# Expert routing in a Hyena and mixture-of-experts layer: where the first weight split runs, where one of three counts runs, and where the first transposes land

## The chip, the cores and the metric

One core of a Trainium2 chip runs the whole program in one launch. The metric is the device time of one execution in microseconds (us), lower is better. Three executions of the kernel before the change took 4108.78, 4110.93 and 4116.41 us; the median is 4110.93.

## The reference, cut to what matters

The program is one layer of a trunk over 2048 latent tokens of width 1024: a Hyena long convolution, a residual and a norm, then a mixture of 16 experts in which each expert chooses its tokens. The change touches the beginning of the second half, which computes this:

```
aff = softmax(h @ w_router)                    # 2048 tokens x 16 experts
gate, idx = top_k(transpose(aff), 256)         # each expert takes its 256 best tokens
xe = h[idx]                                    # gather
ye = (silu(xe @ w1) * (xe @ w3)) @ w2 * gate   # per expert, d_ff = 2048
out[idx] += ye                                 # scatter-add
```

All inputs and outputs are float32.

## The kernel before

**Order of the work.** The layer's first half ends in `phase_out`, which writes the normed tokens to `xnd` in HBM and leaves the logits `lg` in SBUF (128 partitions x 16 token groups x 16 experts). `phase_route` finds each expert's 256th best score. `phase_moe` then runs the experts one after the other.

**Routing.** `lg` becomes the softmax scores: a maximum, a subtraction, Exp on ACT (L1307), a sum, a division. The scores are transposed, so that 128 partitions hold 16 experts in slices, and are taken as two 16-bit halves `vs[1]` (upper) and `vs[0]` (lower). The 256th best is found two bits at a time, from above: 7 steps on the upper half, 8 on the lower. In a step three candidates `cand` are tried: for each, a count on DVE of the entries that are not below it (L1340, 128x256, with an accumulator), then one matmul with the 0/1 matrix `blkb` that adds up the partitions of an expert (L1342), then on DVE the three sums are compared with the capacity (L1358) and the next candidates are formed (L1362). Beside that DVE keeps the threshold `thr` (L1348) and the base of the next candidates (L1355). A step begins when the step before has its `cand`, so the 15 steps form a chain. After them come a running count along the tokens (L1379), two matmuls, and the table `tab` of slots.

**First expert.** `route(0)` makes a one-hot matrix, multiplies it with the table (L1484), computes the token numbers `idx`, and issues two gathers on POOL's queue (L1492, 128 rows of 4 KB each, `xg0` and `xg1`). In four rounds the gathered tokens are transposed on PE into one PSUM bank `tp` (four 128x128 transposes a round, L1502), ACT writes the upper part of the split (`xs` L1504) and DVE the rest (L1505).

**Weights.** Every float32 matrix is split into an upper and a lower part: ACT casts the upper part (`w1h`, `w3h`, `w2h`, L1420), another engine subtracts (`w1l`, `w3l`, `w2l`, L1421). An expert's weights come in 8 chunks of three 1 MB loads (w1, w3, w2) on SP's queue (L1411); raw w1 and w3 have two buffers, raw w2 has one, the split parts have two. `moe_start` loads chunks 0 and 1 of expert 0 ahead, and there the subtraction runs on POOL: all six 128x2048 subtractions stand on POOL's queue beside the steps of the routing. For all later chunks it runs on DVE.

**Experts.** In a chunk, `project` forms two groups of 16 matmuls for each half `i` into the banks `ab` (three of them; L1522, L1523), `hidden` splits the product into `hh` and `hl` (L170, L171), and `back` multiplies it by w2 into four accumulator banks (L175 to L177). Outside the parts under `manual_schedule` a list scheduler fixes the order of the instructions on each engine.

Of the kernel before, what the change touches and what calls it, by code (L numbers as in the profile page):

```python
# [12 lines left out]
F32 = mybir.dt.float32  # L13
F32R = mybir.dt.float32r
BF16 = mybir.dt.bfloat16
I32 = mybir.dt.int32
U16 = mybir.dt.uint16
AF = mybir.ActivationFunctionType
OP = mybir.AluOpType
# [4 lines left out]
T = 2048  # L24
# [26 lines left out]
def f_(ap):  # L51
    return ap.bitcast(F32)
# [1241 lines left out]
def phase_route(tc, ident, ones_f, lg, R):  # L1294
# [6 lines left out]
    with ExitStack() as st:  # L1301
        wk = st.enter_context(tc.tile_pool(reuse_waits="tile", name="r_wk", bufs=1))
        ps = st.enter_context(tc.tile_pool(reuse_waits="tile", name="r_ps", bufs=1, space=PSUM))
        mx = wk.tile([128, 16], F32, name="mx")
# [20 lines left out]
        for h in (1, 0):  # L1325
# [10 lines left out]
            for n in steps:  # L1336
                cnt = wk.tile([128, 3], BF16, name="cnt", bufs=2)
                for k in range(3):
                    junk = wk.tile([128, 256], U16, name=f"junk{k}")
                    nc.vector.tensor_scalar(junk, v, cand[:, k:k + 1], 0.0, op0=OP.is_ge, op1=OP.add, accum_out=cnt[:, k:k + 1])  # L1340
                p = ps.tile([128, 3], F32, name="cp", bufs=2)
                nc.tensor.matmul(p, lhsT=blkb, rhs=cnt, start=True, stop=True)  # L1342
# [15 lines left out]
                nc.vector.tensor_scalar(ge, p, CAP - 0.5, 0.0, op0=OP.is_ge, op1=OP.add, accum_out=num)  # L1358
# [37 lines left out]
def moe_start(tc, A, st, R):  # L1396
# [46 lines left out]
    for n in range(8):  # L1443
        for k in range(3):
            nc.gpsimd.memset(R.kc[:, n, k:k + 1], float((k + 1) << (14 - 2 * n)))
# [6 lines left out]
    R.first = []  # L1452
    for n in range(2):
        R.first.append(split(raws, nc.gpsimd))
        if n == 0:
            raws = load(0, 1)
# [3 lines left out]
def phase_moe(tc, A, rowd, ident, ones_f, lg, R, xnd, accd, out):  # L1460
    nc = tc.nc
    tab, lo, hi, slot, spf = R.tab, R.lo, R.hi, R.slot, R.spf
    with ExitStack() as st:
# [7 lines left out]
        def route(e):  # L1471
# [25 lines left out]
            for q in range(4):  # L1497
                p = ps.tile([128, 2, 256], F32, name="tp", bufs=1)
                for i in range(2):
                    k = 2 * q + i  # L1500
                    for h in range(2):
                        nc.tensor.transpose(out=p[:, i, h * 128:h * 128 + 128], in_=xg[h][:, k * 128:k * 128 + 128], identity=ident)  # L1502
                xh, xl = (xs[:, 2 * q:2 * q + 2, c] for c in range(2))
                nc.scalar.copy(xh, p)  # L1504
                nc.vector.tensor_tensor(xl, p, f_(xh), OP.subtract)  # L1505
                yield
# [102 lines left out]
        with tc.manual_schedule():  # L1609
            for _ in route(0):  # L1610
                pass
# [10 lines left out]
        for e in range(NE - 3):  # L1622
            idx, gate, x = nxt
            acc = [[pa.tile([128, 512], F32, name=f"acc{h}{q}") for q in range(2)] for h in range(2)]
            for fc in range(8):
                ws = R.first.pop(0) if R.first else R.split(R.load(e, fc))
# [202 lines left out]
```

## Time and profile before

The profile below is of one execution of its own.

| | |
|---|---|
| profiled execution | 4111.43 us, of which the span of the profile is 4109.3 us |
| median of three executions | 4110.93 us |
| PE busy | 3840.9 us, 93% of the span |
| DVE busy | 2810.4 us, 68% |
| ACT busy | 1964.7 us, 48% |
| POOL busy | 1092.5 us, 27% |
| granted TensorE clock, mean | 0.972 of 2.4 GHz |
| the 15 routing steps, first count to last matmul | 1801.79 to 1852.86 us of the span |

How to read it: a span time counts from the first instruction. A timeline row gives start, duration, engine, line, operation and, in square brackets, the time that the engine stood idle before it and what ended that. A group row gives the count, the busy time, the mean in ns of one and the idle time before.

### The profile page before, as it was taken

To read this page: it belongs to the slowest core of one execution; us is meant where nothing else is said; L and a number is where in the kernel's file an instruction comes from. 1 tells how busy PE (TensorE), PEld (TensorE's weight loads), DVE (VectorE), ACT (ScalarE), POOL (GpSimd) and SP (SyncE) were. 2 spreads that over 40 slices of the span, in tenths; PEclk is the share of its full clock that TensorE was granted. 3 is DMA by queue.
4 is the path that set the end of the run, shared out by engine and by line. 5 is a ranking of instruction groups with operands and counts; after the bars stand their busy time and mean duration, and the time that the engine had idled before them with its cause. 6 is when DMAs were issued, how large, how long until landed. Compare 5 with 4: busy or idle time off the path is not lost.

```text
span 4109.3 us, 53113 instructions
## 1 busy us (share of the span) xinstructions
PE 3840.9 (93%) x19879; PEld 3185.1 (78%) x19879; DVE 2810.4 (68%) x4018; ACT 1964.7 (48%) x2886; POOL 1092.5 (27%) x1132
## 2 busy tenths in 40 slices
PE   5899999998999998948999999999999999999997
PEld 3666766777777887736888888888888888888896
DVE  5777876776877877785666666666666666656766
ACT  3544543333777652123555555555555555544443
POOL 2355552212577542130000000000000000015635
PEclk8899999999999999968999999999999999999999
DMA  6355656666989995444666666666666666656764
GB/s 200 116 171 171 179 168 210 221 205 220 272 264 268 269 283 190 150 159 149 195 198 202 205 195 198 202 205 195 199 204 205 195 198 207 204 186 213 239 229 161
DMA packets 620797, 831.75 MB, mean 202 GB/s; under 512 B 56627, under 2 KB 506947, under 8 KB 618236
## 3 DMA queue, kind: packets, MB, share of 16 engines
q1 hardware_dynamic: 545594, 661.93, 50.3%
q0 software_dynamic: 57088, 163.48, 13.5%
q10 hardware_dynamic: 17858, 2.95, 0.5%
q8 instruction: 157, 2.57, 0.3%
q14 instruction: 100, 0.82, 0.1%
HBM read 643.82 MB, written 150.75 MB: 193 GB/s over the span
## 4 chain that ended last, share of the span: by engine, by line
PE 72%; DVE 8%; issue 6%; DMA 5%; POOL 4%; ACT 4%; SPq 0%; ACTq 0%; POOLq 0%; DVEq 0%
PE ab L1522 19%; PE ab L1523 10%; PE acc L175 5%; PE acc L176 5%; PE acc L177 5%; PE ip L175 3%; PE ip L177 3%; PE ip L176 3%; PE sp L335 2%; PE op L175 1%; PE op L177 1%; PE op L176 1%; PE xp L857 1%; PE ab L177 1%; PE ab L176 1%
## 5 line engine op out<-in xcount | busy, mean ns | idle before, releaser
L1522 PE MATMUL ab<-xs,w3h 128*128 128x512 f32 x1664 | 600.7, 400 | 0.0
L1522 PE MATMUL ab<-xs,w1h 128*128 128x512 f32 x1664 | 598.3, 399 | 0.0
L1421 DVE TENSOR_TENSOR w2l<-w2r,w2h 128x2048 fp32r<-128x2048 f32 x126 | 297.6, 2362 | 267.2 <-ACT w2h L1420 267.2
L1523 PE MATMUL ab<-xs,w3l 128*128 128x256 f32 x1664 | 468.3, 281 | 0.0
L1523 PE MATMUL ab<-xs,w1l 128*128 128x256 f32 x1664 | 466.6, 280 | 0.0
L175 PE MATMUL acc<-w2h,hh 128*128 128x512 f32 x1024 | 404.2, 395 | 14.7 <-ACT hh L170 13.8
L176 PE MATMUL acc<-w2l,hh 128*128 128x512 f32 x1024 | 402.5, 393 | 0.0
L177 PE MATMUL acc<-w2h,hl 128*128 128x512 f32 x1024 | 399.7, 391 | 0.8 <-DVE hl L171 0.8
L1522 PEld LDWEIGHTS ab<-xs,w3h 128*128 128x128 f32 x1664 | 313.0, 188 | 76.6
L1522 PEld LDWEIGHTS ab<-xs,w1h 128*128 128x128 f32 x1664 | 313.1, 188 | 73.0
L1568 POOL DMA_INDIRECT accd<-y,idx x27 | 68.5, 2536 | 1102.4 <-DVE y L1562 1096.1
L1421 DVE TENSOR_TENSOR w1l<-w1r,w1h 128x2048 fp32r<-128x2048 f32 x126 | 300.9, 2388 | 62.6 <-ACT w1h L1420 62.4
L170 ACT CAST hh<-u 128x256 fp32r<-128x256 f32 x256 | 104.1, 407 | 478.9 <-DVE u L1545 478.9
L1523 PEld LDWEIGHTS ab<-xs,w1l 128*128 128x128 f32 x1664 | 314.2, 189 | 7.1
L1523 PEld LDWEIGHTS ab<-xs,w3l 128*128 128x128 f32 x1664 | 314.8, 189 | 0.0
L1526 DVE TENSOR_TENSOR u<-ab,u 128x256 f32<-128x256 f32 x416 | 174.6, 420 | 204.9 <-ACT u L1525 196.5
L1421 DVE TENSOR_TENSOR w3l<-w3r,w3h 128x2048 fp32r<-128x2048 f32 x126 | 292.9, 2324 | 19.0 <-ACT w3h L1420 19.0
L1420 ACT CAST w2h<-w2r 128x2048 fp32r<-128x2048 f32 x128 | 244.1, 1907 | 95.3 <-PE acc L177 86.5
L1420 ACT CAST w1h<-w1r 128x2048 fp32r<-128x2048 f32 x128 | 244.5, 1910 | 80.0 <-PE ab L1522 78.9
L1420 ACT CAST w3h<-w3r 128x2048 fp32r<-128x2048 f32 x128 | 244.7, 1912 | 68.3 <-PE ab L1522 66.3
L175 PE MATMUL ip<-hh,wh 128*128 128x512 f32 x576 | 239.5, 416 | 2.7 <-ACT hh L170 2.7
L1525 ACT COPY u<-ab 128x256 f32<-128x256 f32 x416 | 153.0, 368 | 184.2 <-PE ab L1523 184.0
(409 smaller groups left out, 9245.2 us busy)
## 6 DMA issues: line engine op xcount, KB each, us to landing
w1r<-in_moe_w_dram SPq DMA_DIRECT2D x128, 1024.0 KB
w3r<-in_moe_w_dram SPq DMA_DIRECT2D x128, 1024.0 KB
w2r<-in_moe_w_dram SPq DMA_DIRECT2D x128, 1024.0 KB
fud<-ev SPq DMA_DIRECT2D x128, 256.0 KB
kr<-fud SPq DMA_DIRECT2D x64, 512.0 KB
bn<-ao POOLq DMA_DIRECT2D x248, 128.0 KB, 7.1
win<-in_c_win_dram SPq DMA_DIRECT2D x64, 256.0 KB
mw<-in_mod_w_dram SPq DMA_DIRECT2D x64, 256.0 KB
```

Source lines behind the costliest of these rows:

```text
L170: nc.scalar.copy(hi, raw)
L175: nc.tensor.matmul(out, lhsT=ah, rhs=bh, start=start, stop=False)
L176: nc.tensor.matmul(out, lhsT=ah, rhs=bl, start=False, stop=False)
L177: nc.tensor.matmul(out, lhsT=al, rhs=bh, start=False, stop=stop)
L335: nc.tensor.matmul(p, lhsT=s1[:, th], rhs=hb[th], start=True, stop=(n0 > 0))
L1420: nc.scalar.copy(h, raw)
L1421: eng.tensor_tensor(l, raw, f_(h), OP.subtract)
L1522: nc.tensor.matmul(p, lhsT=ws[2 * j][:, k, fs], rhs=xs[:, k], start=(k == 0), stop=False)
L1523: nc.tensor.matmul(p[:, 0], lhsT=ws[2 * j + 1][:, k, fs], rhs=xs[:, k, 0], start=False, stop=(k == 7))
L1525: nc.scalar.copy(u, p[:, 1])
L1526: nc.vector.tensor_tensor(u, p[:, 0], u, OP.add)
L1568: nc.gpsimd.indirect_dma_start(out=accd, out_offset=at(idx, h), in_=y, in_offset=None, compute_op=OP.add)
```

## The change

Five edits, all in the routing and in the first chunk of expert 0.

1. POOL no longer subtracts for chunks 0 and 1. Chunk 0's three subtractions run on DVE (as `scalar_tensor_tensor`), called by `R.rest()` behind the issue of the first gathers; chunk 1 is loaded there and split like all later chunks.
2. In each step two counts stay on DVE, now of the entries below the candidate. The third is on ACT: the sign of (candidate - value), summed over the row by the accumulator. The third candidate is lowered by one half so that no difference is zero.
3. The step has two matmuls, one for ACT's sum and one for DVE's two counts, into columns of one bank; the comparison uses a tile of limits `lim` that POOL fills once.
4. `route(0)` puts the first round of transposes into `tp` and the other three into the three banks `ab`.
5. The first chunk takes its split weights from `R.first`, the second its loads from `R.second`.

```diff
+        lim = wk.tile([128, 3], F32, name="lim")
+        nc.gpsimd.memset(lim[:, 0:2], T - CAP + 0.5)
+        nc.gpsimd.memset(lim[:, 2:3], T - 2.0 * CAP + 1.0)
...
-                cnt = wk.tile([128, 3], BF16, name="cnt", bufs=2)
-                for k in range(3):
+                cnt = wk.tile([128, 2], BF16, name="cnt", bufs=2)
+                cs = wk.tile([128, 1], BF16, name="cs", bufs=2)
+                sign = wk.tile([128, 256], BF16, name="sign")
+                with nc.allow_low_precision(reason="whole numbers of at most 256"):
+                    nc.scalar.activation(sign, v, AF.Sign, scale=-1.0, bias=cand[:, 2:3], accum_out=cs)
+                for k in range(2):
                     junk = wk.tile([128, 256], U16, name=f"junk{k}")
-                    nc.vector.tensor_scalar(junk, v, cand[:, k:k + 1], 0.0, op0=OP.is_ge, op1=OP.add, accum_out=cnt[:, k:k + 1])
+                    nc.vector.tensor_scalar(junk, v, cand[:, k:k + 1], 0.0, op0=OP.is_lt, op1=OP.add, accum_out=cnt[:, k:k + 1])
                 p = ps.tile([128, 3], F32, name="cp", bufs=2)
-                nc.tensor.matmul(p, lhsT=blkb, rhs=cnt, start=True, stop=True)
+                nc.tensor.matmul(p[:, 2:3], lhsT=blkb, rhs=cs, start=True, stop=True)
+                nc.tensor.matmul(p[:, 0:2], lhsT=blkb, rhs=cnt, start=True, stop=True)
...
-                nc.vector.tensor_scalar(ge, p, CAP - 0.5, 0.0, op0=OP.is_ge, op1=OP.add, accum_out=num)
+                nc.vector.scalar_tensor_tensor(ge, p, 1.0, lim, op0=OP.mult, op1=OP.is_le, accum_out=num)
...
-    R.first = []
-    for n in range(2):
-        R.first.append(split(raws, nc.gpsimd))
-        if n == 0:
-            raws = load(0, 1)
+    hs = [(n, raw, wt.tile(list(raw.shape), F32R, name=n + "h")) for n, raw in raws]
+    for n, raw, h in hs[:2]:
+        nc.scalar.copy(h, raw)
+
+    def rest():
+        nc.scalar.copy(hs[2][2], hs[2][1])
+        for n, raw, h in hs:
+            l = wt.tile(list(raw.shape), F32R, name=n + "l")
+            nc.vector.scalar_tensor_tensor(l, raw, 1.0, f_(h), op0=OP.mult, op1=OP.subtract)
+            R.first += [h, l]
+        R.second = load(0, 1)
...
-                p = ps.tile([128, 2, 256], F32, name="tp", bufs=1)
+                p = ps.tile([128, 2, 256], F32, name="ab", bufs=3) if wide and q else ps.tile([128, 2, 256], F32, name="tp", bufs=1)
...
-            for _ in route(0):
+            first = route(0, wide=True)
+            next(first), next(first)
+            R.rest()
+            for _ in first:
                 pass
```

ACT, from the last activation of `phase_out` to the loads behind the routing, before (the names carry buffer numbers; the first three casts are chunk 0's, the other three chunk 1's):

```order
L1290 ACTIVATE r_15240<-ident_74 128x1
L1307 ACTIVATE lg_8488<-lg_8488 128x256
L1420 CAST w1h_15258<-w1r_15066 128x2048
L1420 CAST w3h_15262<-w3r_15068 128x2048
L1420 CAST w2h_15266<-w2r_15070 128x2048
L1420 CAST w1h_15276<-w1r_15270 128x2048
L1420 CAST w3h_15280<-w3r_15272 128x2048
L1420 CAST w2h_15284<-w2r_15274 128x2048
```

The same place now, up to the third step's sign:

```order
L1290 ACTIVATE r_15240<-ident_74 128x1
L1465 CAST w2h_15263<-w2r_15070 128x2048
L1310 ACTIVATE lg_8488<-lg_8488 128x256
L1462 CAST w1h_15261<-w1r_15066 128x2048
L1462 CAST w3h_15262<-w3r_15068 128x2048
L1344 ACTIVATE sign_15282,cs_15281<-half1_15276,kc_15077 128x256
L1428 CAST w1h_15785<-w1r_15636 128x2048
L1344 ACTIVATE sign_15302,cs_15301<-half1_15276,cand_15298 128x256
L1428 CAST w3h_15789<-w3r_15638 128x2048
L1344 ACTIVATE sign_15321,cs_15320<-half1_15276,cand_15317 128x256
```

The cast of chunk 0's w2, written behind the gathers in the code, stands ahead of Exp (now L1310); chunk 0's other two casts stand ahead of the first step's sign, and chunk 1's w1 and w3 between the signs of steps 1 and 2 and of steps 2 and 3. The cast of chunk 1's w2 is now in the first chunk of expert 0, behind the first Silu.

DVE, from the second `idx` of expert 0 to the first splits of `xs`, now (before, the four `xs` rows followed the row of `gate` at once):

```order
L1504 TENSOR_TENSOR idx_15613<-tp_15612,n2_15615 128x1
L1505 SCALAR_TENSOR_TENSOR jk_15616,gate_15614<-slot_15075,n2_15615,tp_15612 128x16
L1468 SCALAR_TENSOR_TENSOR w1l_15630<-w1r_15066,w1h_15261 128x2048
L1468 SCALAR_TENSOR_TENSOR w3l_15632<-w3r_15068,w3h_15262 128x2048
L1468 SCALAR_TENSOR_TENSOR w2l_15634<-w2r_15070,w2h_15263 128x2048
L1521 TENSOR_TENSOR xs_15642<-tp_15643,xs_15642 128x2x256
```

Three 128x2048 subtractions now stand between the second gather's index and the first `xs`. On PE all 16 transposes of expert 0 now come in one run, followed by the table matmuls of expert 1 (L1500, before inside expert 0's fourth chunk), and only then the first projection; before, the projection's matmuls stood between the rounds of transposes. Behind expert 0's second chunk the order on every engine is as before.

## Rows read from the trace of the kernel before

**Rows 1.** Windows view, busy us (and instructions) of each engine, then PEclk, DMA share, GB/s.

```profile
1870.00:1880.00 10.00, 8.62 (x43) 7.50 (x44) 2.77 (x4) 2.35 (x4) 0.00 (x0) 0.74 0.01 2
...
1940.00:2500.00 560.00, 559.12 (x2967) 476.46 (x2966) 353.94 (x454) 288.54 (x376) 30.97 (x18) 1.00 0.63 201
```

**Rows 2.** Timeline of the first routing step: start us, us, engine, line, operation.

```profile
1801.22 4.52 POOL L1421 TENSOR_TENSOR w1l<-w1r,w1h 128x2048 fp32r<-128x2048 f32 x1 [43.17 <-ACT w1h L1420]
...
1803.34 2.43 DVE L1355 TENSOR_SCALAR base<-kc,thr 128x3 f32<-128x3 f32 x1
```

**Rows 3.** Groups of instructions, 1640 to 1960 us: busy us, mean ns, idle before.

```profile
L1362 DVE SCALAR_TENSOR_TENSOR cand<-num,base 128x3 f32<-128x3 f32 x13 | 10.5, 806 | 0.5
...
L1355 DVE TENSOR_SCALAR base<-kc,thr 128x3 f32<-128x3 f32 x13 | 9.2, 710 | 0.4
...
L1348 DVE SCALAR_TENSOR_TENSOR thr<-num,thr 128x1 f32<-128x1 f32 x13 | 8.1, 624 | 0.0
```

**Rows 4.** Source view of the same three lines: ns min/median/max.

```profile
L1362 DVE SCALAR_TENSOR_TENSOR cand<-num,base x13: 160/161/4356, 1805.9 to 1851.2; 128x3 f32<-128x3 f32 x13
...
L1355 DVE TENSOR_SCALAR base<-kc,thr x13: 98/228/4425, 1803.3 to 1850.8; 128x3 f32<-128x3 f32 x13
...
L1348 DVE SCALAR_TENSOR_TENSOR thr<-num,thr x13: 152/153/3215, 1811.5 to 1852.6; 128x1 f32<-128x1 f32 x13
```

**Rows 5.** Timeline of the fifth routing step, POOL idle.

```profile
1830.85 0.48 DVE L1340 TENSOR_SCALAR_CACHE_REDUCE junk<-half,cand 128x256 uint16<-128x256 uint16 x1
...
1831.26 0.47 DVE L1340 TENSOR_SCALAR_CACHE_REDUCE junk<-half,cand 128x256 uint16<-128x256 uint16 x1
...
1832.20 0.16 PE L1342 MATMUL cp<-cnt,blkb 128*128 128x3 bf16 x1 [1.78 <-DVE junk L1340]
```

**Rows 6.** Timeline: Exp on ACT, the first step's first count on DVE, two casts of chunk 1 on ACT.

```profile
1798.95 0.40 ACT L1307 ACTIVATE lg<-lg 128x256 f32<-128x256 f32 x1
...
1801.79 0.48 DVE L1340 TENSOR_SCALAR_CACHE_REDUCE junk<-half,kc 128x256 uint16<-128x256 uint16 x1
...
1805.86 1.90 ACT L1420 CAST w1h<-w1r 128x2048 fp32r<-128x2048 f32 x1 [1.11 <-DMA w1r<-in_moe_w_dram]
...
1808.86 1.90 ACT L1420 CAST w3h<-w3r 128x2048 fp32r<-128x2048 f32 x1 [1.11 <-DMA w3r<-in_moe_w_dram]
```

**Rows 7.** Groups of instructions on ACT, whole span, shapes kept apart.

```profile
L526 ACT ACTIVATE ht<-g,md 128x256 f32<-128x256 f32 x48 | 24.2, 565 | 18.8 <-DMA h2d<-ht 8.0 <-issue 5.2 <-DVE hl L530 3.5
...
L1290 ACT ACTIVATE r<-ident 128x1 f32<-128x1 f32 x1 | 0.2, 203 | 0.0
```

**Rows 8.** Timeline: the two gathers of expert 0 and the transposes that wait.

```profile
1862.27 1.18 POOL L1492 DMA_INDIRECT xg<-xnd,idx  x1 [34.25 <-DVE jk L1489]
...
1863.76 0.97 POOL L1492 DMA_INDIRECT xg<-xnd,idx  x1 [0.30 <-issue]
...
1869.03 0.90 PE L1502 MATMUL tp<-ident,xg 128*128 128x128 f32 x3 [1.76 <-DMA xg<-xnd,idx]
```

**Rows 9.** Timeline in expert 0: a DVE subtraction and a scatter of POOL beside it.

```profile
2024.41 2.28 DVE L1421 TENSOR_TENSOR w1l<-w1r,w1h 128x2048 fp32r<-128x2048 f32 x1
2024.45 3.68 POOL L1568 DMA_INDIRECT accd<-y,idx  x1 [6.18 <-DVE y L1562]
```

**Rows 10.** Source view of the scatters (ns min/median/max) and of the gathers' landing.

```profile
L1568 POOL DMA_INDIRECT accd<-y,idx x27: 1602/1654/3717, 2016.6 to 3947.1; - x27
...
DMA to landing us min/median/max: 4.4/5.7/9.7
```

**Rows 11.** Timeline late in the experts: a small POOL instruction, and the second of two DVE subtractions in a row.

```profile
3691.26 2.20 POOL L1594 TENSOR_SCALAR t<-t 128x2 f32<-128x2 f32 x1
3693.32 2.28 DVE L1421 TENSOR_TENSOR w3l<-w3r,w3h 128x2048 fp32r<-128x2048 f32 x1
```

**Rows 12.** Timeline of PE and ACT in expert 0's first chunk.

```profile
1871.38 1.11 PE L1502 MATMUL tp<-ident,xg 128*128 128x128 f32 x4 [1.45 <-DVE xs L1505]
...
1880.28 0.37 ACT L1525 COPY u<-ab 128x256 f32<-128x256 f32 x1 [1.78 <-PE ab L1523]
```

More of the change, by code (lines that the diff above doesn't have):

```diff
@@ L1444, in moe_start @@
         for k in range(3):
-            nc.gpsimd.memset(R.kc[:, n, k:k + 1], float((k + 1) << (14 - 2 * n)))
+            nc.gpsimd.memset(R.kc[:, n, k:k + 1], float((k + 1) << (14 - 2 * n)) - 0.5 * (k == 2))
     nc.gpsimd.iota(ii, pattern=[[1, 128]], base=128, channel_multiplier=-1)
@@ L1451, in moe_start @@
     yield
-    R.first = []
-    for n in range(2):
-        R.first.append(split(raws, nc.gpsimd))
-        if n == 0:
-            raws = load(0, 1)
+    hs = [(n, raw, wt.tile(list(raw.shape), F32R, name=n + "h")) for n, raw in raws]
[8 more added lines that the diff above has]
+        R.second = load(0, 1)
+    R.first, R.rest = [], rest
     yield
@@ L1469, in phase_moe, with route @@
         ps = st.enter_context(tc.tile_pool(reuse_waits="tile", name="e_ps", bufs=2, space=PSUM))
-        def route(e):
+        def route(e, wide=False):
             oh = wk.tile([128, 256], F32, name="oh", bufs=1)
@@ L1625, in phase_moe @@
             for fc in range(8):
-                ws = R.first.pop(0) if R.first else R.split(R.load(e, fc))
+                ws = R.first if e + fc == 0 else R.split(R.second if e + fc == 1 and e == 0 else R.load(e, fc))
                 for i in range(2):
```

## The prediction

> **What bounds the kernel now.** I read the windows first. In the experts PE is the bound: it is busy 559.12 of 560 us between 1940 and 2500 us [rows 1], so what delays the first projection delays the end by as much. Ahead of that lies the routing, where PE does almost nothing and DVE is the chain: 15 steps, each waiting for the last. So the question is how much earlier expert 0's first projection can start. The timeline of the first steps shows what is slow there: POOL starts a 4.52 us subtraction of weights at 1801.22, and DVE's `base`, three numbers a partition, starts at 1803.34 and ends at 1805.77, 0.03 us after POOL's subtraction [rows 2]. DVE waits for POOL. The groups by line show how much that is in all, and the source view what the same instructions take undisturbed. About 0.2% of the time, 8 us, is what a measurement here can tell from no change.
>
> **Part 1: no subtraction on POOL beside the steps.** The lines `cand`, `base` and `thr` were busy 10.5 + 9.2 + 8.1 = 27.8 us, 13 instructions each [rows 3]. At their medians, 161, 228 and 153 ns [rows 4], they would take 13 x 0.542 = 7.05 us. Six of the 39 instructions carry the difference. All of it lies on the chain. **-20.75 us.** The bounds are close: the counts themselves did not stretch.
>
> **Part 2: a count fewer on DVE.** Two counts start 0.41 us apart, I take 0.40; a step lasts 1.94 us, the matmul's 0.16 and the 1.78 that PE idles before it; 1.35 of that lies between the first count and the matmul, so the next first count comes 0.6 us behind the matmul [rows 5]. A step becomes 1.54 us if nothing else ends later. 15 x 0.40: **-6.0 us.** ACT's sign must not end later than two counts, 0.9 us. No ACT instruction with an accumulator is in the trace. Nearest is an activation of the same 128x256 with a column as its bias, 0.57 us, and for a possible read of the accumulator one of 128x1, 0.20 us [rows 7]: 0.77 us at most by these rows, 0.57 if the read is hidden; I take 0.7. Its matmul, 0.16 us, then ends when DVE's counts do. Ends: 0 to 0.1 us a step, so 0 to +1.5 us in all. The new comparison has the same 128x3 shape, and I cost it at nothing; a 0.05 us surcharge a step would be 0.75 us.
>
> **Part 3: ACT's queue in the first three steps.** This is given back, and only the order shows it. Three casts of 1.90 us and two loads now stand ahead of or between the signs.
> - Chunk 0's w2 cast stands ahead of Exp. Exp, which ended at 1799.35, and with it the first count, 1801.79 [rows 6], come 1.9 us later, at 1801.25 and 1803.7, if that load has landed by then. +1.9.
> - The casts of chunk 0's w1 and w3 follow Exp; each takes 1.9 us, and 0.1 of it overlaps. So the first sign starts at 1804.85 and ends at 1805.55, while the two counts end at 1804.6. +0.95.
> - Step 2 begins near 1806.2. ACT first casts chunk 1's w1, which cannot start before its load lands at 1805.86 [rows 6], so the sign starts at 1807.76 and ends at 1808.45; the counts end at 1807.1. +1.35.
> - Step 3 begins at 1809.1. Chunk 1's w3 lands at 1808.86 [rows 6]; its cast ends at 1810.76, the sign at 1811.45, the counts at 1810.0. +1.45.
> - Against that, the clearing of `seg` on DVE in step 3 is now hidden by the wait: -0.4.
>
> Sum **+5.2 us**. The ends: +3.3 if Exp were not held, +14.3 if the w2 load landed late (a rival below). POOL's two memsets of the limits lie beside the softmax and cost nothing, for the first comparison comes 4 us later.
>
> **Part 4: the gathers beside DVE's subtractions.** Before, DVE was free behind the indices. Now its three subtractions, 2.3 us each, begin, behind the few small instructions of the second index, by estimate 0.75 us after POOL starts the first gather. Call that start T. The second gather begins at T + 1.49, takes 0.97 us, and the transposes that need it start at T + 6.76, 4.3 us behind its end [rows 8]. What a DVE subtraction does to such an instruction is in the trace: a scatter that POOL started 0.04 us behind one took 3.68 us and ended 1.44 us behind the subtraction's end [rows 9], where the shortest takes 1.60 us [rows 10]. So the second gather's instruction runs after the first subtraction, at T + 3.05, and ends near T + 4.0 instead of T + 2.46: +1.5. Its data then move beside the load of chunk 2's w1, which SP issues when that subtraction has freed the buffer. Gathers beside weight loads land after 5.7 us in the median, 9.7 at most, the start of the instruction being zero [rows 10], against 5.3 here: +0.5, ends 0 and +4.4. Sum **+2.0 us**. The Trainium skill, page "SBUF — State Buffer", section "Who interferes with whom", says that a tensor_tensor takes only the shared read interface and infers that writing descriptors needs the write interface, hence no stall of a DMA. By that the +1.5 would be 0 and the time 4089.4. The scatter's 3.68 us contradicts it, so the measured price stays in the sum. The subtractions themselves end at T + 7.6, before the first `xs` on DVE, which waits for ACT behind the transposes: they cost nothing.
>
> **Part 5: four banks.** Before the second round of transposes PE idled 1.45 us for DVE to empty the single bank [rows 12]; the other rounds had matmuls between them. Now the 16 transposes run in one piece and the gap goes: -1.45. The table matmuls of expert 1 move to there, where PE has the lower clock, and vanish later: I take +0.45 for the difference. **-1.0 us**, ends 0 and -2.5 (an unbroken run might bring the higher clock sooner). What else moved: ACT and DVE do chunk 1's subtractions and w2 cast in the time of PE's chunk 0. That is the load of every later chunk, with which DVE is busy 354 and ACT 289 of 560 us while PE never waits [rows 1], so I cost it at nothing; `hh` of the first half now stands behind three casts, and PE meets it about when it is ready.
>
> **Sum.** -20.75 - 6.0 + 5.2 + 2.0 - 1.0 = -20.55. Against the profiled execution's 4111.43 that is 4090.9, rounded **4091**; the median of the three runs is 0.5 lower than that execution, which is less than their spread.
>
> **Rivals.**
> - **The gather is starved by all three subtractions**: POOL's instruction comes through only at T + 7.6, 4.55 us later than above: 4095.5. For it: the three stand back to back, and a gather may need the port more than once. Against it: between two such subtractions POOL got in: its two-column instruction of 3691.26 was held 2.20 us and ended at 3693.46, while the second subtraction had begun at 3693.32 and took its usual 2.28 [rows 11]. Chance 0.09.
> - **Exp waits for the load.** The w2 load was issued with five others behind it. If they share the engines evenly, it lands with the last, at 1808.86. Exp is then 9.8 us later than in part 3, and step 4 starts some 9 us later, the other casts no longer waiting: 4100. Against it: the two loads that do show a landing came 3.0 us apart [rows 6], one after the other. Chance 0.07.
> - **The lead of the weights was what counted.** POOL had two chunks split before PE began; now there is one, and chunk 1's w2 is loaded behind everything. ACT meets its cast behind the first copy of `u`, which before came 11.25 us behind the transposes' start [rows 8, 12], so near T + 20. Three loads of 3.0 us from T + 3.1 land by about T + 14. To cost 12 us, so that the change would not be seen, the last would have to land near T + 32. At a whole chunk, 88 matmuls or 16.6 us at 560/2967 us each [rows 1], it is 4107. Chance 0.07.
> - **Slower: TensorE's clock.** PE rises from 1.2 to 2.4 GHz in the first chunk; 1870 to 1880 was granted 0.74, later stretches 1.00 [rows 1]. The change alters what PE does just then. If the lower level stayed, PE's work would take up to twice as long, losing up to half of every microsecond; from 41 us of it the gain is gone, and 70 us would give 4126. Against it: PE was as busy there and got 1.00 afterwards. Chance 0.03.
>
> **Numbers.** Forecast 0.74, rivals 0.09, 0.07, 0.07, 0.03. Faster by over 0.2%: the forecast and the first two, 0.90 (4100 is 11 us faster); within: 0.07; slower: 0.03. Below, the ends add up to -5.4 (gather not held or crowded -2.0, clock -1.5, Exp not held -1.9), which gives 4086; above to +6.2 (sign +1.5, comparison +0.75, gather crowded +3.9), 4097. To 4101 the range takes in the first two rivals; outside lie the other two, 0.10, and as much again for what I have not seen.
>
> **What would show it.** `cand`, `base` and `thr` without a duration over 0.3 us; step 4's first count near 1812; twelve steps at 1.54 us; the second gather's POOL instruction at 2.4 us or more; first `w2` cast ahead of Exp without idle time before it. Wrong it is if PE waits in chunks 1 or 2 for weights, if a step lasts over 1.7 us (the sign is then the chain), or if the gathers' instruction lasts past 6 us.

## The result, and the profile after

Five executions of the changed kernel took 4089.07 to 4092.57 us, median 4091.15. Five of the kernel before, on the same chip, had a median of 4110.93. The ratio is 0.9948, with a 95% interval from 0.9936 to 0.9960: faster, by 19.8 us.

The profiled execution took 4092.45 us, of which 4090.7 are the span; the granted clock was 0.977 of 2.4 GHz in the mean (before 0.972). Up to the routing the two programs do the same work (two small fills on POOL aside), but their executions differ: the routing's first reduction on DVE began at 1797.56 us before and at 1799.20 after. So 1.64 us were lost where nothing was changed. From there to the end of the span it is 2311.74 us before and 2291.50 after, 20.2 less. That start is the zero of every "mark" below.

The page's first part, after (share of the span, instructions):

```profile
PE 3849.8 (94%) x19894; PEld 3190.2 (78%) x19894; DVE 2795.3 (68%) x3994; ACT 1972.8 (48%) x2916; POOL 1071.5 (26%) x1128
```

PE has nearly the same work in a shorter span. The source view of the routing's lines after (ns min/median/max) answers to [rows 4]:

```profile
L1370 DVE SCALAR_TENSOR_TENSOR cand<-num,base x13: 161/163/164, 1807.4 to 1832.3; 128x3 f32<-128x3 f32 x13
L1370 DVEq EVENT_SEMAPHORE  x11: 21/21/21, 1813.2 to 1832.2; - x11
...
L1363 DVE TENSOR_SCALAR base<-kc,thr x13: 105/228/229, 1806.4 to 1831.8; 128x3 f32<-128x3 f32 x13
...
L1356 DVE SCALAR_TENSOR_TENSOR thr<-num,thr x13: 152/154/156, 1808.5 to 1833.3; 128x1 f32<-128x1 f32 x13
...
L1344 ACT ACTIVATE sign<-half,cand x13: 504/507/509, 1809.2 to 1832.6; 128x256 bf16<-128x256 uint16 x13
L1344 ACT ACTIVATION_READ_ACCUMULATOR sign<-half,cand x13: 188/189/190, 1809.6 to 1833.0; 128x1 bf16 x13
```

The maxima of 3.2 to 4.4 us are gone: none of these lines waits for POOL any more. The sign takes 0.51 us, its accumulator is read by an instruction of its own of 0.19. The second row is new: in 11 of 13 steps a separate waiting instruction stands ahead of `cand`.

The timeline of ACT after, from the cast ahead of Exp to the third sign, and DVE's first counts of steps 4 and 5:

```profile
1800.59 1.88 ACT L1465 CAST w2h<-w2r 128x2048 fp32r<-128x2048 f32 x1
1802.38 0.41 ACT L1310 ACTIVATE lg<-lg 128x256 f32<-128x256 f32 x1
...
1806.28 0.50 ACT L1344 ACTIVATE sign<-half,kc 128x256 bf16<-128x256 uint16 x1
...
1807.42 1.90 ACT L1428 CAST w1h<-w1r 128x2048 fp32r<-128x2048 f32 x1 [0.54 <-DMA w1r<-in_moe_w_dram]
...
1810.35 1.90 ACT L1428 CAST w3h<-w3r 128x2048 fp32r<-128x2048 f32 x1 [0.53 <-DMA w3r<-in_moe_w_dram]
1812.15 0.50 ACT L1344 ACTIVATE sign<-half,cand 128x256 bf16<-128x256 uint16 x1
...
1813.51 0.48 DVE L1347 TENSOR_SCALAR_CACHE_REDUCE junk<-half,cand 128x256 uint16<-128x256 uint16 x1
1815.13 0.48 DVE L1347 TENSOR_SCALAR_CACHE_REDUCE junk<-half,cand 128x256 uint16<-128x256 uint16 x1
```

Exp starts 3.18 us behind the zero instead of 1.39. The first step begins at 1805.23, the fourth at 1813.51: 8.28 us for three steps, since the first sign stands behind two casts of chunk 0 and the next two each behind a cast that waits for its load. From there a step lasts 1.62 us.

The timeline of the first gathers after, with SP's load (SPq is its queue) and PE; it answers to [rows 8, 12]:

```profile
1842.93 1.18 POOL L1508 DMA_INDIRECT xg<-xnd,idx  x1 [44.92 <-DVE jk L1505]
1843.59 2.29 DVE L1468 SCALAR_TENSOR_TENSOR w1l<-w1r,w1h 128x2048 fp32r<-128x2048 f32 x1
1844.41 2.32 POOL L1508 DMA_INDIRECT xg<-xnd,idx  x1 [0.30 <-issue]
1845.94 0.37 SPq L1419 DMA_DIRECT2D w1r<-in_moe_w_dram  x1
...
1852.49 0.90 PE L1518 MATMUL tp<-ident,xg 128*128 128x128 f32 x3 [4.56 <-DMA xg<-xnd,idx]
1853.18 2.77 PE L1518 MATMUL ab<-ident,xg 128*128 128x128 f32 x12
1855.74 0.68 PE L1500 MATMUL tp<-tab,oh 128*128 128x33 f32 x4
1856.25 0.47 PE L1538 MATMUL ab<-xs,w1h 128*128 128x512 f32 x1
```

The second gather's instruction lasts 2.32 us instead of 0.97, beside DVE's subtraction. The transposes that need its rows start 9.56 us behind the first gather's start, 2.80 later than before. Then they run in one piece. Behind that PE waits for nothing: the windows view (as [rows 1]) of expert 0 and what follows:

```profile
1860.00:1960.00 100.00, 100.00 (x529) 85.36 (x528) 63.78 (x80) 52.32 (x68) 3.01 (x2) 1.00 0.66 219
1960.00:2500.00 540.00, 540.00 (x2864) 460.36 (x2864) 343.47 (x428) 281.30 (x365) 29.10 (x16) 1.00 0.62 199
```

The marks, us behind the zero, from one profiled execution of each kernel. T is the start of the first gather on POOL; the next two columns are the start of the last three transposes of round one and of the first projection, behind T; the last is the start of the first `y`, when expert 0 is through.

| kernel | Exp | last step done | T | transposes - T | projection - T | expert 0 through |
|---|---|---|---|---|---|---|
| before | 1.39 | 55.74 | 64.71 | 6.76 | 9.88 | 217.40 |
| changed | 3.18 | 34.81 | 43.73 | 9.56 | 13.32 | 197.04 |
| changed, second execution (r0) | 3.18 | 34.75 | 43.67 | 9.51 | 13.34 | 197.01 |
| a1 chunk 0 on POOL | 1.38 | 46.19 | 55.10 | 6.73 | 10.70 | 206.11 |
| a2 three counts on DVE | 3.18 | 36.67 | 45.64 | 9.79 | 13.76 | 199.90 |
| a3 one bank | 3.18 | 34.85 | 43.77 | 9.67 | 12.74 | 200.74 |
| b1 subtractions behind gathers | 3.18 | 34.82 | 43.74 | 6.99 | 10.95 | 195.36 |
| b2 casts behind steps | 1.39 | 29.84 | 38.75 | 9.51 | 13.48 | 192.58 |
| b4 fresh candidates | 3.17 | 33.40 | 42.31 | 9.96 | 13.92 | 196.55 |
| b5 lock without load | 3.18 | 34.77 | 43.69 | 7.20 | 11.21 | 195.57 |
| b6 load without lock | 3.18 | 34.91 | 43.82 | 7.94 | 11.91 | 195.99 |
| c2 = b1 + b2 + b4 | 1.39 | 28.86 | 37.77 | 6.89 | 10.86 | 188.99 |
| c4 = c2, three counts on DVE | 1.39 | 34.87 | 43.85 | 6.83 | 10.80 | 195.23 |

Before and a3 run projections between the rounds of transposes, so their sixth column starts earlier for no gain.

### The profile page after: what moved, and what is told of

The parts are those of the page before. It is cut to its first block, busy times and chain, and to the rows that moved or that the text cites. A ratio compares the mean times of both kernels' runs of the same rounds, so it can differ in the third digit from the quotient of the medians.

```text
span 4090.7 us, 53171 instructions
## 1 busy us (share of the span) xinstructions
PE 3849.8 (94%) x19894; PEld 3190.2 (78%) x19894; DVE 2795.3 (68%) x3994; ACT 1972.8 (48%) x2916; POOL 1071.5 (26%) x1128
## 4 chain that ended last, share of the span: by engine, by line
PE 72%; DVE 8%; issue 6%; DMA 5%; POOL 5%; ACT 4%; SPq 0%; ACTq 0%; POOLq 0%; DVEq 0%
PE ab L1538 19%; PE ab L1539 10%; PE acc L175 5%; PE acc L176 5%; PE acc L177 5%; PE ip L175 3%; PE ip L177 3%; PE ip L176 3%; PE sp L335 2%; PE op L175 1%; PE op L176 1%; PE op L177 1%; PE xp L857 1%; PE ap L892 1%; PE xp L875 1%
```

## The experiments

The question was which part the 20 us came from, whether the parts that cost something cost it where the prediction said, and whether those costs can be had back. Whole times of one kernel spread over 2 to 13 us. The zero itself lies between 1790.52 and 1807.04 us in the thirteen profiled executions of the table, in work that no edit touches. So terms of 1 to 3 us are read from the marks, and the times are a coarse check. A chip's own time of the kernel before is what a run's time is held against. The kernel before took 4112.74 us on the chip of a1 to b1, 4113.05 on that of r0, b2, b4 and c2, 4111.00 for b5 and c4, 4112.56 for b6.

### a1: chunk 0's subtractions back on POOL

```diff
-    for n, raw, h in hs[:2]:
-        nc.scalar.copy(h, raw)
+    for n, raw in raws:
...
+        nc.scalar.copy(h, raw)
+        nc.gpsimd.tensor_tensor(l, raw, f_(h), OP.subtract)
...
     def rest():
-        nc.scalar.copy(hs[2][2], hs[2][1])
...
         R.second = load(0, 1)
```

> Chunk 0's three subtractions go back to POOL beside the routing steps (and its w2 cast ahead of the first sign, as in the kernel before); chunk 1 stays as in the changed kernel. Theory: DVE's small instructions wait for POOL's 4.5 us subtractions. Six of them cost 20.75 us before, so three cost about 10.4, of which up to 2.5 us may hide in the first three steps, which wait for ACT anyway. Given back: the gathers are alone on the port, POOL's second gather lasts about 0.97 us instead of 2.32 and the first transposes start 6.8 us behind the first gather instead of 9.6 (-2.8). Exp is not held by the w2 cast, but the first sign is (about -0.5 together). Sum: 4095 to 4099 us, three of cand, base and thr over 3 us. Rival (the waits were not what the change saved, the count and the banks were): no long cand, base or thr, and 4089 or less.

Measured: 4100.76 us, ratio 0.9973 (0.9962 to 0.9983). Timeline of the run, POOL and DVE:

```profile
1801.93 4.51 POOL L1465 TENSOR_TENSOR w1l<-w1r,w1h 128x2048 fp32r<-128x2048 f32 x1 [4.86 <-ACT w1h L1464]
...
1803.64 2.83 DVE L1363 TENSOR_SCALAR base<-kc,thr 128x3 f32<-128x3 f32 x1
...
1806.58 4.35 DVE L1370 SCALAR_TENSOR_TENSOR cand<-num,base 128x3 f32<-128x3 f32 x1
...
1811.77 3.62 DVE L1356 SCALAR_TENSOR_TENSOR thr<-num,thr 128x1 f32<-128x1 f32 x1
...
1815.56 2.29 DVE L1429 TENSOR_TENSOR w1l<-w1r,w1h 128x2048 fp32r<-128x2048 f32 x1
...
1817.84 2.29 DVE L1429 TENSOR_TENSOR w3l<-w3r,w3h 128x2048 fp32r<-128x2048 f32 x1
...
1824.80 2.28 DVE L1429 TENSOR_TENSOR w2l<-w2r,w2h 128x2048 fp32r<-128x2048 f32 x1
```

Three long instructions, one of each line, as expected. Over their medians they lose 2.60 + 4.19 + 3.47 = 10.26 us where 10.4 were expected. The first step, which holds two of them, lasts 8.47 us, as long as the first step before the change. So the rival (the waits were not what counted) is out.

The marks and the time of this run do not price the waits alone, for the edit moved more than its text says. The last three rows are chunk 1's subtractions on DVE: the scheduler has put them into steps 2 and 5, where the changed kernel has none, and they make these steps some 6.4 us longer (9.27 us without the wait of 3.47 and a plain step of 1.55, and 3.73 against 1.62). On the other side Exp starts 1.8 us earlier than in the changed kernel, and no step waits for ACT, worth 3.2 (8.28 us for the first three steps there, 5.03 in c2). 10.3 + 6.4 - 1.8 - 3.2 = 11.7, and the last step is done 11.4 us later. Expert 0 is through 9.1 later, since the gather, alone again, gives 2.8 back. The time, 4100.76, lies 1.8 us above the 4095 to 4099 that were expected, which left chunk 1's subtractions out; on this chip the kernel before was 1.8 us slower, too (4112.74 against 4110.93).

Which instructions wait fits a statement of the Trainium skill, page "SBUF — State Buffer", section "Who interferes with whom": a tensor_scalar can take the pair of ports that DVE shares with POOL, but not the form that also writes its accumulator, and an instruction with two SBUF inputs contends, too. Here `base`, a tensor_scalar without an accumulator, was held 2.83 us, while all 30 counts of the run, which have one, took 473 to 480 ns.

### a2: three counts on DVE, the new comparison kept

```diff
-                nc.scalar.activation(sign, v, AF.Sign, scale=-1.0, bias=cand[:, 2:3], accum_out=cs)
-                for k in range(2):
+                for k in range(3):
```

> All three counts on DVE again, with the new comparison kept; all else as in the changed kernel. Theory: ACT's casts ate most of what the sign gave. In the changed kernel the 15 steps take 8.28 us for the first three and 1.62 for each of the others, 27.7 in all; with three counts no step waits for ACT. If the 0.08 us that a step lasts over the predicted 1.54 come from the new form of comparison, a step lasts 1.94 + 0.08 = 2.02 us, all 15 take 30.3 and the time is 2.6 higher: 4093.7. Rival: the 0.08 us come from the sign, its read and the second matmul; then a step lasts 1.94, all 15 take 29.1 and the time is 4092.5. Second rival: the sign is worth its 6.0 us net; then 4097.

Measured: 4094.74 us, ratio 0.9956 (0.9939 to 0.9973); the last step is done 1.86 us later than in the changed kernel. A step lasts 1.945 us, as before the change. The timeline of one step, DVE:

```profile
1827.69 0.16 DVE L1360 SCALAR_TENSOR_TENSOR ge<-cp,lim 128x3 f32<-128x3 f32 x1
...
1827.89 0.16 DVE L1364 SCALAR_TENSOR_TENSOR cand<-num,base 128x3 f32<-128x3 f32 x1
```

From `ge` to `cand` it is 0.20 us with the new comparison; in the changed kernel it was 0.28 (1827.15 to 1827.43). So the comparison costs nothing (the first rival's numbers) and the missing 0.08 us a step come with the sign. And with the casts in its way the sign, all its steps together, was worth 1.9 us at the last step. Expert 0 is through 2.9 us later; the other 1.0 arose behind the steps, in the landing of the gather and the first chunks, where executions differ by as much.

### b4: 14 buffers for the candidates

The program's order with its waits shows what differs: in the changed kernel (first row) the instruction that writes `cand` waits for DVE and for ACT, because the sign of two steps ago has to have read the buffer; in b4 (second row), and in a2, it waits for DVE alone.

```
L1370 SCALAR_TENSOR_TENSOR cand_15357<-num_15355,base_15352 128x3 [waits DVE_49,Activation_49]
L1370 SCALAR_TENSOR_TENSOR cand_15357<-num_15355,base_15352 128x3 [waits DVE_49]
```

```diff
-                    cand = wk.tile([128, 3], F32, name="cand", bufs=2)
+                    cand = wk.tile([128, 3], F32, name="cand", bufs=14)
```

> The candidates get 14 buffers instead of 2, so that writing them waits for no earlier sign of ACT; all else as in the changed kernel. The run with three counts on DVE had the new comparison and a step of 1.94 us, so the comparison's form costs nothing. Theory: the 0.08 us a step are those of the second wait (on ACT, long satisfied) of the instruction that writes the candidates: from the start of ge to that of cand 0.20 us instead of 0.28, a step 1.54 us, time 1.0 to 1.2 lower, 4090.0. Rival: the 0.08 us belong to the second matmul or to ACT's accumulator: 0.28, 1.62 and 4091.2 as before.

Measured: 4090.75 us, ratio 0.9945 (0.9930 to 0.9960), beside r0's 4091.59. Timeline and source view of the run:

```profile
1828.89 0.16 DVE L1366 SCALAR_TENSOR_TENSOR ge<-cp,lim 128x3 f32<-128x3 f32 x1
...
1829.10 0.16 DVE L1370 SCALAR_TENSOR_TENSOR cand<-num,base 128x3 f32<-128x3 f32 x1
```

```profile
L1370 DVE SCALAR_TENSOR_TENSOR cand<-num,base x13: 160/161/163, 1810.3 to 1833.7; 128x3 f32<-128x3 f32 x13
```

0.21 us from `ge` to `cand`, a step of 1.545 us, no waiting instruction on the line any more, and the last step 1.41 us earlier: 0.9 are the 11 waits, 0.2 a step of 1.82 us that the changed kernel has in both its executions and b4 has not, the rest a second step of 2.43 instead of 2.86 us, where ACT waits for a load. At the end of expert 0 only 0.5 us of it are left, for here the transposes came 0.4 us later behind T, and from there on it took 0.5 longer. The wait's condition had long been met; the wait itself was the price. The Trainium skill, page "Perfetto Trace Analysis", section "Identifying Dependency Chains", says that a wait on several engines may be given EventSemaphore instructions ahead of it; the trace agrees, and the price here was 0.08 us a step, four times the 21 ns that the row shows.

### b2: the casts behind the steps

```diff
-    for n, raw, h in hs[:2]:
-        nc.scalar.copy(h, raw)
+    def casts():
+        for n, raw, h in hs:
+            nc.scalar.copy(h, raw)
+        R.early = [(raw, wt.tile(list(raw.shape), F32R, name=n + "h")) for n, raw in load(0, 1, slice(0, 2))]
+        for raw, h in R.early:
+            nc.scalar.copy(h, raw)
...
+        R.casts()
         tv = wk.tile([128, 1], I32, name="tv")
```

> ACT's five casts (chunk 0's three, chunk 1's w1 and w3) stand behind the last of the 15 signs, where ACT is idle; all else as in the changed kernel. Theory: the casts ahead of Exp and between the signs cost the chain 1.8 us (Exp) and 3 x 1.62 = 4.9 instead of 8.28 us in the first three steps (-3.4): first gather 38.5 us behind the start of the routing instead of 43.7, time 5.2 lower, 4086.0. The casts end 9.5 us behind the last sign and so after about the first gather's start; w1's is done long before DVE subtracts. Rival: the subtractions or chunk 1 now meet an unfinished cast; DVE's three subtractions then show waits for ACT, PE waits in chunk 1, and the time is 4089 or more.

Measured: 4086.85 us, ratio 0.9935 (0.9920 to 0.9951). T is 4.98 us earlier, expert 0 through 4.46 earlier. The three first steps take 1.67, 1.55 and 1.89 us; the third is longer because clearing `seg` on DVE, 0.48 us, is on the chain again, as the prediction had it. DVE's three subtractions show no wait for ACT, and the time is not the rival's 4089 or more.

### b1, b5 and b6: what holds up the gather

b1 lets DVE subtract only when POOL is through with both gathers:

```diff
+        one = R.kc[:, 0, 0:1]
+        nc.gpsimd.memset(one, 1.0)
...
-            nc.vector.scalar_tensor_tensor(l, raw, 1.0, f_(h), op0=OP.mult, op1=OP.subtract)
+            nc.vector.scalar_tensor_tensor(l, raw, one, f_(h), op0=OP.mult, op1=OP.subtract)
```

> DVE's three subtractions read a column that POOL writes behind the second gather's instruction, so they begin only when POOL is through with it; w2's stands behind the four splits of the gathered tokens. Theory: with DVE quiet POOL's second gather lasts about 0.97 us instead of 2.32, and the data, ahead of the load of chunk 2's w1, land as before the change: first transposes 6.8 to 7.3 us behind the first gather's start instead of 9.6, time 4088.4 to 4088.9. Rival A: only the instruction is held by the port and the data are slow because of the loads in any case: 8.2 us, 4089.8. Rival B: the subtractions, which now end about 2 us later against the gather, hold the first split on DVE: the gain is lost, 4091 or more.

Measured: 4085.79 us, ratio 0.9930 (0.9914 to 0.9947). Transposes at T + 6.99, the first projection 2.37 us earlier, expert 0 through 1.68 earlier. The theory's number for the transposes holds. The time is lower than the marks account for; in the profiled execution 3.5 us of that lie ahead of the zero. But b1 moves two things: what holds POOL's second gather while DVE subtracts (the lock, for short), and the load of chunk 2's w1, which needs the buffer that the first subtraction frees. b5 and b6 part them. b5 is b1 with one more subtraction on DVE at once behind the indices:

```diff
+            if n == "w1":
+                nc.vector.scalar_tensor_tensor(f2(l), f2(hs[2][1]), 1.0, f2(f_(hs[2][2])), op0=OP.mult, op1=OP.subtract)
```

> As the run with the subtractions behind the gathers, but one more subtraction, whose result is overwritten, stands on DVE at once behind the second index, and chunk 1's w1 follows it: DVE works from 0.7 to about 5.2 us behind the first gather's start, while the next load of weights is issued only at about 5.2 us, as late as in that run (5.0) and not at 3.0 as in the changed kernel. The changed kernel's gather landed 5.8 us behind POOL's instruction, which ended at 3.8; alone it lands 4.3 to 4.5 behind it. Theory (the load takes the 1.4 us): POOL's second gather lasts 2.3 us and the transposes start 3.8 + 4.4 = 8.2 us behind the first gather's start. Rival (DVE's work itself slows the landing, too): 9.5 us, as in the changed kernel.

b6 is b1 with a load that nothing needs (other lines of its edit are left out; up to the gathers ACT and SP work as in the changed kernel):

```diff
+            nc.scalar.activation(gf, R.w2raw.rearrange("p a b -> p (a b)"), AF.Identity, bias=nxt_gate[0][:, 1:2])
+            nc.sync.dma_start(gf.rearrange("p (k f) -> p k f", k=8), A["moe_w1"][0].rearrange("e (k p) f -> e p k f", p=128)[0, :, :, 512:768])
```

> The converse of the last but one run: the subtractions wait behind the gathers, so DVE is quiet and POOL's second gather lasts 0.97 us, but a 1 MB load of weights that nothing needs, chunk 2's w1 into the tile that later holds the norm's gains, is issued about 2.8 us behind the first gather's start (the changed kernel issued its load at 3.0, the run with the subtractions behind the gathers at 5.0). That run with a locked POOL and the load at 5.2 had the transposes at 7.2 us. Theory: the load alone takes the gathered rows' time; transposes at 9.0 us or more, as in the changed kernel (9.5). Rival: it needs both, the lock and the load, or the lock moves the descriptors behind the load: 7.2 us or less.

Measured: b5 4090.51 us, 0.9950 (0.9932 to 0.9968); b6 4088.98, 0.9939 (0.9917 to 0.9962). Timelines of the second gather, the next load and the transposes, b5 and then b6 (T is 1843.60 and 1842.18):

```profile
1845.08 2.32 POOL L1515 DMA_INDIRECT xg<-xnd,idx  x1 [0.30 <-issue]
...
1848.82 2.59 SPq L1419 DMA_DIRECT2D w1r<-in_moe_w_dram  x2
...
1850.80 0.90 PE L1525 MATMUL tp<-ident,xg 128*128 128x128 f32 x3 [2.07 <-DMA xg<-xnd,idx]
```

```profile
1843.66 0.97 POOL L1514 DMA_INDIRECT xg<-xnd,idx  x1 [0.30 <-issue]
...
1845.07 0.37 SPq L1639 DMA_DIRECT2D gb<-in_moe_w_dram  x1
...
1850.12 0.90 PE L1524 MATMUL tp<-ident,xg 128*128 128x128 f32 x3 [2.62 <-DMA xg<-xnd,idx]
```

Neither theory nor rival of b5 had its number: locked for 2.32 us, with the load at T + 5.2, the rows still land at T + 7.20, 0.2 us later than unlocked (b1). The instruction's end is not what the landing counts from. In b6 the load alone, at T + 2.89, makes it 7.94, 0.95 later than b1: less than the theory said, more than the rival. Both together, as in the changed kernel, make it 9.51 to 9.56, 2.5 later (9.5 to 10.0 in the other runs that leave this place alone). So the two don't add.

The trace's DMA view, which counts the packets of each queue by their start, shows why. q0 carries the two gathers (256 packets of 4 KB), q1 the loads. Queue, packets, MB and share of the engines between T + 4 and T + 6, for the changed kernel, b5 and b6:

```profile
q1 hardware_dynamic: 374, 0.38, 70.1%
q0 software_dynamic: 6, 0.00, 0.2%
```

```profile
q0 software_dynamic: 88, 0.35, 71.5%
```

```profile
q0 software_dynamic: 120, 0.43, 76.1%
q1 hardware_dynamic: 84, 0.09, 14.7%
```

In the changed kernel the load, issued 0.8 us ahead of the end of POOL's instruction (1845.94 to 1846.73), has these 2 us nearly to itself: its packets start at T + 4.01, those of the second gather only at T + 6.06 (by the starts of single packets in the same trace), 2.26 us behind the instruction's end. Locked without the load (b5) they start at T + 4.50, unlocked (b1) at T + 3.93, close behind the first gather's. In b6 they start at T + 4.02, ahead of the load's (T + 4.92), and only the last of them are late. So the lock costs little by itself, but it moves the second gather's packets behind the start of the load's. By which rule the gather's packets then wait is not shown by any run and stays open.

### a3: one bank

```diff
-            first = route(0, wide=True)
+            first = route(0)
```

> The four rounds of transposes share the one bank tp again, all else as in the changed kernel. Theory (the prediction's): PE waits 1.45 us again ahead of the second round, less what the table matmuls cost at the lower clock; from the first transpose to the first matmul of back it takes 18.3 us instead of 17.3, and the time is 4092.2. Rival: the split of the gathered tokens on ACT and DVE sets the pace of the first projection either way: 17.3 us and 4091.2, no change.

Measured: 4093.22 us, ratio 0.9954 (0.9938 to 0.9971). From the transposes to the end of expert 0 it is 147.3 us instead of 143.75 (marks): 3.5 us, more than the theory's 1.0. PE's timeline of the run, and its windows from 4 us behind the transposes' start on, then windows of the changed kernel from 2 us behind them on, then from 4 to 6 us in b1 and in the kernel before:

```profile
1849.40 1.12 PE L1518 MATMUL tp<-ident,xg 128*128 128x128 f32 x4 [1.40 <-DVE xs L1521]
...
1860.23 0.50 PE L1538 MATMUL ab<-xs,w1h 128*128 128x512 f32 x1 [0.78 <-DVE xs L1521]
```

```profile
1851.10:1853.10 2.00, 2.00 (x8) 1.71 (x7) 2.00 (x3) 0.04 (x1) 0.00 (x0) 0.50 0.77 260
1853.10:1855.10 2.00, 2.00 (x11) 1.77 (x11) 1.24 (x1) 0.24 (x1) 0.00 (x0) 0.70 0.90 262
```

```profile
1854.50:1856.50 2.00, 2.00 (x12) 2.00 (x11) 1.62 (x3) 1.47 (x3) 0.00 (x0) 0.61 1.08 387
1856.50:1858.50 2.00, 2.00 (x13) 1.75 (x13) 1.89 (x2) 0.07 (x1) 0.00 (x0) 1.00 0.65 248
```

```profile
1850.44:1852.44 2.00, 2.00 (x8) 1.71 (x9) 1.89 (x2) 0.08 (x1) 0.00 (x0) 0.53 1.05 363
```

```profile
1873.03:1875.03 2.00, 2.00 (x8) 1.71 (x8) 0.69 (x1) 0.09 (x1) 0.00 (x0) 0.50 0.05 8
```

The gap of 1.40 us is back, and a second one of 0.78 appears ahead of the last round's projections. The granted clock (PEclk, the figure behind POOL's) was 0.50, the level of 1.2 GHz, between 4 and 6 us behind the transposes' start and 0.70 in the next 2 us; in the changed kernel it was 0.61 between 2 and 4 us and 1.00 from 4 us on. So one bank costs 2.2 us of gaps here, and a later rise of the clock on top. But the time of the rise does not follow from the gap: in b1, whose transposes were unbroken as well, 1.00 came 6 us behind their start, and about as late in the kernel before, which had the gap. What sets it was not found.

### c2 and c4: the three together, and what the sign is then worth

> The three together: subtractions behind the gathers, casts behind the steps, 14 buffers for the candidates. If the three places are independent, the gains add: 5.2 (casts) + 1.2 (buffers) + 2.6 (gather) = 9.0 us, 4082.2 where the changed kernel takes 4091.2. Rival: with the routing 6.5 us shorter, ACT's casts (9.5 us in a row) end behind the point where DVE may begin, or chunk 2's loads come late; then less than 6 us, 4085 or more, and DVE's first subtraction shows a wait for ACT.

c2 joins the edits of b1, b2 and b4. Measured: **4084.68 us**, ratio 0.9933 (0.9920 to 0.9947), beside 4091.59 for the changed kernel on the same chip: 6.9 us faster. Expert 0 is through 8.05 us earlier than in the changed kernel, T 5.96 earlier, the transposes 2.67 earlier against T. The casts run behind the last sign and end before DVE needs them; the first one and the last, and DVE's first subtraction, which waits for POOL's column and not for ACT:

```profile
1824.67 1.88 ACT L1464 CAST w1h<-w1r 128x2048 fp32r<-128x2048 f32 x1
...
1831.86 1.90 ACT L1467 CAST w3h<-w3r 128x2048 fp32r<-128x2048 f32 x1
...
1837.14 2.35 DVE L1474 SCALAR_TENSOR_TENSOR w1l<-w1r,kc,w1h 128x2048 fp32r<-128x2048 f32 x1 [1.85 <-POOL kc L1471]
```

It beats both kernels. By whole times it is not told apart from b1 alone (ratio 0.9930, interval 0.9914 to 0.9947); that the casts and the buffers add their part rests on the marks, 188.99 against 195.36. The expected sum of the three, 9.0, was not quite reached: the 0.3 us of `seg` come back with the casts gone, and where the gather lands early part of its gain is lost again to the low clock. In b1 the first projection starts 2.37 us earlier and expert 0 is through only 1.68 earlier; 4 to 6 us behind the transposes' start the clock was 0.53 there and 1.00 in the changed kernel.

> As the run with all three, but with the three counts on DVE: what the sign is worth once ACT's casts are out of its way. Theory (the prediction's term): 0.40 us a step, 15 steps, 6.0 us: the last step ends 34.9 us behind the start of the routing instead of 28.9, the time is 4090.7 where the run with all three takes 4084.7. Rival: ACT's casts of chunk 0, which now start right behind Exp, or the landing of the gather make up for part of it; 4088 or less.

c4 is c2 with a2's edit. Measured: 4090.00 us, ratio 0.9948 (0.9934 to 0.9962). The last step is done at 34.87 instead of 28.86: 6.01 us, the prediction's 6.0 for this part. Expert 0 is through 6.2 us later. The rival is out. The sign is worth its full 6 us only where ACT has nothing else to do; in the changed kernel it was 1.9 (a2).

### r0: the changed kernel once more

> The changed kernel itself once more, on the chip of the next three runs, so that their stretches can be laid beside it: 4091 us where the kernel before takes 4111; steps 4 to 8 of 1.62 us each; the second gather on POOL 2.3 us; the four first transposes 9.6 us behind the first gather's start if the slow landing of the gathered rows belongs to the kernel, 8.2 us if it was an accident of the profiled execution.

Measured: 4091.59 us, ratio 0.9954 (0.9939 to 0.9969); steps of 1.62 us, 2.32 us on POOL, transposes at T + 9.51. The slow landing belongs to the kernel.

## Why the prediction was right, point by point

Forecast 4091, measured 4091.15, range 4086 to 4101. The forecast case came true. That it came within 0.15 us is luck: single terms were off by up to 1.2 us, and the profiled execution lost 1.64 us ahead of the routing, in work that the change does not touch. Against the zero, at the end of expert 0:

| term | predicted | measured |
|---|---|---|
| 1 waits for POOL | -20.75 | -20.84 |
| 2 a count fewer | -6.0 | -4.92 |
| 3 ACT's queue | +5.2 | +4.87 |
| 4 gathers beside subtractions | +2.0 | +2.80 |
| 5 four banks | -1.0 | -2.18 |
| sum | -20.55 | -20.27 (marks: 197.04 - 217.40 = -20.36) |

Terms 4 and 5 are measured by place, up to the transposes and from there on. Undone alone, term 4 gives back 1.68 us at the end of expert 0 (b1) and term 5 costs 3.7 (a3).

1. **Right, and its cause is shown.** The 39 instructions went from 27.8 us [rows 3] to 13 x (163 + 218 + 154) ns = 7.0, and a1, with half of the subtractions on POOL, loses 10.26 us in three of them.
2. **Mechanism right, size off by 1.1 us.** The step is 1.62, not 1.54: 15 x (1.945 - 1.617) = 4.9. The new comparison, priced at nothing with a bound of 0.05, costs nothing (a2). What the prediction missed is that `cand` now waits for two engines, +0.08 in 11 steps; the waits that stand with the order of the program showed it. The other 0.2 is the one step of 1.82 us. Without the second wait the step is 1.545 (b4) and the whole part 6.01 (c4 against c2). The sign's 0.7 us was close: 0.60 from its start to the end of its read.
3. **Right.** +1.8 for Exp (3.18 against 1.39), +3.4 for the first three steps (8.28 against 3 x 1.62), -0.34 for `seg` (1.89 against 1.55 us in b2). The first `w2` cast stood ahead of Exp without idle time, step 4 began at 1813.51, 1811.9 without the late start, where 1812 was forecast.
4. **The sum near, its inside wrong.** The instruction behaved as forecast: through at T + 3.80, forecast T + 4.0. But the step that let the instruction end near T + 4.0 instead of T + 2.46 and priced this at +1.5 took the instruction's end for the data's landing, and b5 shows that by itself this is worth 0.2. What was called crowding and priced at 0.5 is the larger part, 0.95 alone (b6) and 2.5 together with the lock. The rule of the Trainium skill that the prediction weighed here (page "SBUF — State Buffer", section "Who interferes with whom") gave 0 for the lock: wrong for the instruction, which took 2.32 us, but near the truth for what the lock by itself does to the data.
5. **Right in sign, too small.** -2.2 from the transposes to the end of expert 0 (145.93 before, 143.75 after), beside other edits there. The gap of 1.45 is gone. How much comes on top goes with the time at which the clock rose: in b1, where it rose about as late as before, the same stretch took 144.6, a gain of 1.3, close to the forecast. The rest is the sooner clock that the prediction had only as an end of its range, -2.5; r0 had it too (0.58 and then 1.00 in the same two windows), and why it came sooner is open.

The rivals: the gather was not starved (2.32 us, not 4.5 more); the cast of w2 ahead of Exp met a landed load; PE waited for no weights in chunks 1 and 2 (100.00 of 100 us busy), so the shorter lead cost nothing; the clock rose sooner, not later (1.00 from 4 us behind the transposes' start, 0.50 there before).

## What to carry to other kernels

An engine that is idle in the share of busy time may not be idle where work is moved to: look at its order around that place, for here the scheduler had filled such gaps with casts and loads, and pin those behind the chain. The same goes for an experiment: a1's edit also moved three subtractions of DVE into the chain, and only the rows could tell the two apart. Count the engines that each instruction on a serial chain waits for; another buffer can be cheaper than a wait that is always met. And a longer DMA-issuing instruction is not yet a later transfer: look at when its packets start and land, and at what else moves then.

## What the runs showed of the hardware that was not expected

- A second wait, long met, cost 0.08 us on DVE: 0.28 us from `ge` to `cand` with it, 0.20 without.
- POOL's gather instruction lasted 2.32 us instead of 0.97 beside a DVE instruction with two SBUF inputs, and its rows landed 0.2 us later only (T + 7.20 against 6.99), until a 1 MB load was issued 0.8 us before its end: then 2.5 later, the load's packets starting at T + 4.01 and the gather's at T + 6.06.
- The granted clock reached 1.00 4 us behind the start of unbroken transposes in the changed kernel and 6 in b1; where a gap broke them it was 6 in the kernel before and 8 in a3.
